# Decay matrices of a chunked scan: dt and the mask moved into the exponent, masking and the sum of both directions on GpSimd

## The chip, the core and the metric

The kernel runs on one core of a Trainium2 chip. A core has five engines that work side by side, each through a queue of its own in a fixed order: TensorE (PE in the profile; PEld is its loading of weights), VectorE (DVE), ScalarE (ACT), GpSimd (POOL) and SyncE (SP), which here only issues transfers. They wait for each other through semaphores. The metric is the device time of one launch in microseconds; less is better.

## The reference, cut to what matters

One layer of a diffusion backbone: 512 latent tokens, 256 context tokens, width 1024, one input projection, a convolution branch, a bidirectional Mamba-2 scan with 32 heads in 8 groups, an output projection and an MLP. The change touches the scan inside chunks of 128 tokens only:

```python
cum = jnp.cumsum(dts * a, axis=2)
xdt = x5 * dts[..., None]
seg = cum_t[..., :, None] - cum_t[..., None, :]
lower = jnp.tril(jnp.ones((q, q), dtype=bool))
decay = jnp.exp(jnp.where(lower, seg, -jnp.inf))
cb = jnp.einsum('bcqgn,bckgn->bcgqk', cs_, bs)
y_diag = jnp.einsum('bcgrqk,bckgrp->bcqgrp', cb[:, :, :, None] * decay, xdt)
...
y_off = jnp.einsum('bcqgn,bcgrpn,bcqgr->bcqgrp', cs_, h_in, jnp.exp(cum))
```

Both directions are added, the backward one with the upper triangle as its mask. For each head and chunk the kernel so needs the matrix M[k, q] = cb[k, q] * sum over the two directions of mask * exp(cum_q - cum_k) * dt_k.

## The kernel before

Tokens lie along the free axis, channels on the partitions. Every large product is done as three passes over exact high and low halves (`gemm`, L114 to L116): a weight tile of 128 columns and all 1024 channels takes 24 products. Its weights come by one transfer (`raw`, L96), ScalarE makes the high half (`whi`, L105), VectorE the low half (`wlo`, L106), with two buffers for each. The tile framework lists the instructions of every engine in an order of priority; `later(n)` moves what is traced inside it. That order is fixed when the program is built: each engine takes its instructions strictly one after the other.

After the conditioning and the first norms, `dt_part` (L294 to L359) computes dt and the running sums cf of dt times a for all 64 head-directions, writes cf and exp(cf) to a scratch in DRAM (`s_cf`), and turns wg, cf and dt to token-by-partition form (`wgT`, `cfT`, `dtT`). Then come eight groups. For group g, `proj(g)` makes B, C, X and Z of the group (six weight tiles; `taps5`, L374, runs the short convolution on VectorE straight out of PSUM), and `ssd(g, ...)` does the scan. Beside groups 0 to 4, `glu` and `taps` run a tile of the convolution branch, whose 30 taps per tile (L575) are all on VectorE. After group 7 come three more of these tiles, the gates, LayerNorm, and the projections.

Inside `ssd`: `cps` holds cb of the four chunks (L442) and VectorE multiplies it with a mask for each direction (`cbm`, L446). B and x are transposed (`bps`, `xps`), x is weighted (`xw`, L470), the states that enter the chunks are built (`sps`, `hst`, L485 to L498). Then for j = 0, 1 there is a pair of heads, r = 0, 1, with one PSUM tile `yps`. For each head and direction d:

- SP fetches cf and exp(cf) of this head, spread over all partitions, into `cfb` (L507, 3 buffers).
- ScalarE makes relu(cf_k - cf_q) chunk by chunk (L510, four instructions; the per-token cf is the bias), and exp(-that) (L512, one instruction) into `e`.
- VectorE multiplies with the masked `cbm` (L513).
- dt: for d = 0 ScalarE scales the four chunks (L517), for d = 1 VectorE multiplies and adds onto the first direction (L520, four instructions). The tile of d = 0 is then M.
- `Cd` = C times exp(cf) (L523): one of four on VectorE, three on GpSimd.

M tiles come from the tag "M" with three buffers, so the fourth head of a group writes where the group's first head stood. TensorE does 16 products of `Cd` and `hst` (L536) and 8 of M and `xt` (L532) for each `yps` tile, each 64 x 128. The two heads of a pair fill the two halves of PSUM's partitions. The trace counts every such f32 product as two instructions, so 32 and 16. What follows is `yt` (L540, L541), its store and its square sum (GpSimd, L548).

Of the kernel before, what the change touches and what calls it, by code (L numbers as in the profile page):

```python
# [8 lines left out]
F32 = mybir.dt.float32  # L9
F32R = mybir.dt.float32r  # L10
BF16 = mybir.dt.bfloat16
AF = mybir.ActivationFunctionType
ALU = mybir.AluOpType
# [13 lines left out]
# columns of the packed per-channel vectors  # L27
# [8 lines left out]
# order of the input projection's 128-column tiles  # L36
# [6 lines left out]
# the groups beside which the first tiles of the convolution module run  # L43
GLU_AT = (0, 1, 2, 3, 4)
# the steps of the first modulation vectors beside which the first three weight tiles come, and ctx
BEGIN_AT, CTX_AT = (0, 1, 2), 3
# products that keep the tensor engine's clock up before there is work
WARM = 22
# the products of C and the decays (direction, head of the pair) that VectorE does, the rest are GpSimd's
DECAYS_V = ((0, 1),)  # L50
# how far instructions move in the order of priority
# [5 lines left out]
def build(tc, xT, ctxT, cond, crow, wada1, wada2, vecs, hv, cst, w_in, w_co, w_so, w_o, w_1, w_2, outT):  # L57
    nc = tc.nc
    with ExitStack() as es:
# [8 lines left out]
        C = cp.tile([P, 4, P], F32, name="C")  # L68
        ident, ones, mask_f, mask_b = (C[:, i, :] for i in range(4))

# [15 lines left out]
        @contextmanager  # L86
        def later(n):
            """what is traced inside gives way to the next n instructions"""
            tc.cur_priority += n
            yield  # L90
            tc.cur_priority -= n

# [37 lines left out]
        def rsqrt_mean(ps, n, cnt, r=None):  # L130
            """1/sqrt(sum/cnt + EPS) of a sum broadcast over the partitions"""
# [18 lines left out]
        def rsqrt_rows(parts, n, cnt, pool, out=None):  # L150
            """the same of the sum of several tiles, found token by token and then spread over the partitions"""
# [40 lines left out]
        with tc.tile_pool(name="st", bufs=1) as st:  # L192
# [31 lines left out]
            # products of nothing: the tensor engine's clock halves when it idles  # L224
# [52 lines left out]
        nc.sync.dma_start(C[:, 2:], cst[:, 2:])  # L277
# [7 lines left out]
        H2 = 2 * HEADS  # L285
        cfT = cp.tile([P, NCH, H2], F32, name="cfT")
        dtT = cp.tile([P, NCH, H2], F32, name="dtT")
# [6 lines left out]
        def dt_part(ps, pc):  # L294
            conv = bigt("conv")
            # rows: heads forward, the same again, heads backward, the same again; the first of each hold
            # chunks 0 to 2, the second chunk 3 and the context
# [10 lines left out]
            # softplus: max(v, 0) + log1p(u), u = exp(-|v|), log1p(u) = 2 atanh(u / (2 + u))  # L308
# [13 lines left out]
            # running sums within the chunks and within the context, backward ones from the end  # L322
# [15 lines left out]
            nc.vector.tensor_tensor(wg, wg, dt_, ALU.mult)  # L338
            nc.scalar.activation(ecf, cf, AF.Exp)
# [5 lines left out]
            # step s: chunk s forward, chunk 3 - s backward  # L345
# [4 lines left out]
            for src, dst in ((wg, wgT), (cf, cfT), (dt_, dtT)):  # L350
                pt = pm.tile([P, T], F32, name="dtp", tag="pm")
                for c in range(3):
                    nc.tensor.transpose(pt[:, c * P:(c + 1) * P], src[:, c * P:(c + 1) * P], ident)
                pv = pt[:, :L].rearrange("p (c d w h) -> p c d w h", c=3, d=2, w=2)
                dv = dst.rearrange("p c (d h) -> p c d h", d=2)
                nc.scalar.copy(dv[:, :3], pv[:, :, :, 0])
                n = dst.shape[1] - 3
                nc.scalar.copy(dv[:, 3:], pv[:, :n, :, 1])
            return conv  # L359

# [26 lines left out]
        def xbc_first():  # L387
            """the first group's, all of x's part before ctx's"""
# [24 lines left out]
        cacc = acct("cacc")  # L413

# [22 lines left out]
        def ssd(g, Bt, Ct, X, Z):  # L437
            ch = lambda t, c: t[:, c * P:(c + 1) * P]
            # B^T C of every chunk, for both directions
# [3 lines left out]
            cbm = []  # L443
            for m in (mask_f, mask_b):
                t = spool.tile([P, NCH, P], F32, name="cbm", tag=f"cbm{len(cbm)}", bufs=1)
                nc.vector.tensor_tensor(  # L446
                    t, cps.rearrange("p (c q) -> p c q", q=P), m.unsqueeze(1).broadcast_to([P, NCH, P]), ALU.mult)
                cbm.append(t)
            # B by token
# [6 lines left out]
            # x by token, and times what reaches the chunk's end  # L456
# [21 lines left out]
            # states that enter the chunks: step s is chunk s forward, chunk 3-s backward  # L478
# [20 lines left out]
            # outputs of the heads, two to a PSUM tile  # L499
            for j in range(2):  # L500
                yps = py.tile([P, T], F32, name="yps", tag="py")
                Ms, Cs = [], ([], [])
                for r in range(2):
                    for d in range(2):
                        hd = d * HEADS + 4 * g + 2 * j + r
                        cb_ = spool.tile([P, 2, T], F32, name="cfb", tag="cfb", bufs=3)
                        nc.sync.dma_start(cb_, s_cf[hd].unsqueeze(0).broadcast_to([P, 2, T]))  # L507
                        e = (spool if d else tp).tile([P, T], F32, name="e", tag="e" if d else "M", bufs=2 if d else 3)
                        for c in range(NCH):
                            nc.scalar.activation(  # L510
                                ch(e, c), cb_[:, 0, c * P:(c + 1) * P], AF.Relu, bias=cfT[:, c, hd:hd + 1], scale=-1.0)
                        nc.scalar.activation(e, e, AF.Exp, scale=-1.0)  # L512
                        nc.vector.tensor_tensor(e, e, cbm[d].rearrange("p c q -> p (c q)"), ALU.mult)  # L513
                        if d == 0:
                            M = e
                            for c in range(NCH):
                                nc.scalar.activation(ch(M, c), ch(M, c), AF.Copy, scale=dtT[:, c, hd:hd + 1])  # L517
                        else:
                            for c in range(NCH):
                                nc.vector.scalar_tensor_tensor(  # L520
                                    ch(M, c), ch(e, c), dtT[:, c, hd:hd + 1], ch(M, c), ALU.mult, ALU.add)
                        Cd = (spool if d else tp).tile([P, T], F32, name="Cd", tag="Cd", bufs=4 if d else 3)
                        (nc.vector if (d, r) in DECAYS_V else nc.gpsimd).tensor_tensor(Cd, Ct, cb_[:, 1, :], ALU.mult)  # L523
                        Cs[d].append(Cd)
                    Ms.append(M)
# [178 lines left out]
        def four_w(srcs, hpool, lpool, name):  # L704
            """four weight tiles that stay"""
# [10 lines left out]
        def sumsq(j, a, b, wcol):  # L716
            """squares of channel tile j added up; the last tile's by themselves"""
# [9 lines left out]
        def with_norm(srcs, rhs, gcol, keep, finish, wcol=None):  # L727
            """x1 += gate * product; the last four tiles by halves of the tokens, so that each half's
            norm runs beside the next products"""
# [74 lines left out]
def _layout(inp):  # L804
# [33 lines left out]
    i = np.arange(P)  # L838
    cst = np.stack([np.eye(P), np.ones((P, P)), i[:, None] <= i[None, :], i[:, None] >= i[None, :]], 1)
# [37 lines left out]
```

## Time and profile before

Three timed runs: 1263.3, 1263.39 and 1267.06 us, median 1263.39. The profiled execution has a span of 1264.2 us from its first to its last instruction; no other time of that execution is given.

| what | value |
|---|---|
| median of the timed runs | 1263.39 us |
| span of the profiled execution | 1264.2 us |
| mean granted TensorE clock | 0.991 |
| scan with the group projections (about 100 to 620 us) | 520 us |
| GpSimd in it | 67 instructions, 102.6 us busy |
| loads of ScalarE's function tables, L512 alone | 28, 35.9 us |

A row of a group of instructions reads: line, engine, operation, tile written <- tiles read, shapes, count | busy time, mean ns of one | idle time of the engine just before them, with what ended it. In a timeline a row is: start, duration, engine, line, operation, count, and in brackets the idle time before it and what ended that. A busy TensorE is not TensorE at its peak, since products are pipelined: how dense it is can be read from the distance of the starts, not from the durations.

### The profile page before, as it was taken

What the parts mean: (1) busy time and instruction counts of PE and PEld (TensorE: products, weight loads), DVE (VectorE), ACT (ScalarE), POOL (GpSimd) and SP (SyncE); (2) the same over time, 40 slices, a digit from 0 to 9 for tenths busy, and PEclk for the clock granted to TensorE, in tenths of its full rate; (3) what the DMA queues carried; (4) which work ended last, traced back from release to release, by engine and by line L of the source; (5) the groups of instructions that cost most, each with busy time, mean ns of one, the idle gap of its engine ahead of it and who ended that gap; (6) DMA issues with size and microseconds to landing.
All of it is one profiled execution on the core that took longest, in us unless ns stands there. A gap on an engine that the chain in (4) does not pass through costs nothing.

```text
span 1264.2 us, 17493 instructions
## 1 busy us (share of the span) xinstructions
PE 1220.7 (97%) x6665; PEld 995.6 (79%) x6665; DVE 953.7 (75%) x1567; ACT 667.4 (53%) x1124; POOL 108.9 (9%) x74
## 2 busy tenths in 40 slices
PE   6998999999999899999999999999999999999997
PEld 3786778777787778787888877778998888888886
DVE  6797689999999999998999798885843343443444
ACT  4557888686776748868453452134431331331442
POOL 0001222121020302124000000000000000000000
PEclk8999999999999999999999999999999999999999
DMA  9424363343342424333363357964222333233332
GB/s 363 142 67 133 137 198 128 120 146 106 121 159 93 158 83 147 112 134 117 109 193 126 119 188 258 305 196 153 62 65 86 100 100 92 92 100 101 96 104 67
DMA packets 56260, 169.96 MB, mean 134 GB/s; under 512 B 6640, under 2 KB 9584, under 8 KB 56048
## 3 DMA queue, kind: packets, MB, share of 16 engines
q1 hardware_dynamic: 56176, 168.85, 41.0%
q8 instruction: 52, 0.85, 0.3%
q14 instruction: 32, 0.26, 0.1%
HBM read 162.27 MB, written 6.55 MB: 134 GB/s over the span
## 4 chain that ended last, share of the span: by engine, by line
PE 65%; DVE 20%; DMA 8%; issue 3%; ACT 3%; SPq 0%; POOL 0%; DVEq 0%; ACTq 0%; POOLq 0%
PE ps L114 20%; PE ps L115 19%; PE ps L116 19%; DVE conv L575 5%; DVE wlo L106 3%; DVE Xt L374 3%; DMA aw<-in_wada_dram 2%; DMA cfb<-s_cf 2%; PE yps L536 2%; PE yps L532 2%; PE sps L485 1%; DMA yr<-s_y 1%; DVE aw L675 1%; DMA raw<-in_w_dram 1%; ACT whi L105 1%
## 5 line engine op out<-in xcount | busy, mean ns | idle before, releaser
L105 ACT CAST whi<-raw 128x1024 fp32r<-128x1024 f32 x163 | 170.9, 1049 | 320.6 <-PE ps L115 291.5
L106 DVE TENSOR_TENSOR wlo<-raw,whi 128x1024 fp32r<-128x1024 f32 x163 | 203.8, 1251 | 84.3 <-ACT whi L105 76.1
L114 PE MATMUL ps<-hh,whi 128*128 128x512 f32 x632 | 258.0, 408 | 2.3 <-DVE Xt L374 2.1
L116 PE MATMUL ps<-hh,wlo 128*128 128x512 f32 x632 | 255.4, 404 | 2.3 <-DVE wlo L106 2.2
L115 PE MATMUL ps<-hl,whi 128*128 128x512 f32 x632 | 256.7, 406 | 0.0
L575 DVE SCALAR_TENSOR_TENSOR conv<-sg,V,conv 128x480 f32<-128x480 f32 (+14 forms) x240 | 173.3, 740 | 2.6 <-ACT conv L569 1.1
L114 PEld LDWEIGHTS ps<-hh,whi 128*128 128x128 f32 x632 | 119.4, 189 | 30.8 <-issue 7.2
L116 PEld LDWEIGHTS ps<-hh,wlo 128*128 128x128 f32 x632 | 119.4, 189 | 30.7 <-DVE wlo L106 4.7
L115 PEld LDWEIGHTS ps<-hl,whi 128*128 128x128 f32 x632 | 119.6, 189 | 26.5 <-issue 3.7
L711 DVE SCALAR_TENSOR_TENSOR x<-ps,mod,x 128x512 f32<-128x512 f32 (+1 forms) x48 | 31.7, 660 | 100.1 <-PE ps L116 100.1
L510 ACT ACTIVATE e<-cfb,cfT 128x128 f32<-128x128 f32 x256 | 83.9, 391 | 36.8 <-PE yps L532 17.5
L523 POOL TENSOR_TENSOR Cd<-Ct,cfb 128x512 f32<-128x512 f32 x48 | 72.6, 1518 | 313.0 <-DMA cfb<-s_cf 250.3
L116 PE MATMUL ps<-h2h,wlo 128*128 128x512 f32 (+1 forms) x240 | 89.8, 375 | 0.0
L115 PE MATMUL ps<-h2l,whi 128*128 128x512 f32 (+1 forms) x240 | 89.8, 375 | 0.0
L114 PE MATMUL ps<-h2h,whi 128*128 128x512 f32 (+1 forms) x240 | 89.4, 375 | 0.0
L115 PE MATMUL ps<-gl,whi 128*128 128x512 f32 x224 | 88.4, 395 | 0.0
L114 PE MATMUL ps<-gh,whi 128*128 128x512 f32 x224 | 88.2, 394 | 0.0
L116 PE MATMUL ps<-gh,wlo 128*128 128x512 f32 x224 | 87.9, 392 | 0.0
L374 DVE SCALAR_TENSOR_TENSOR Xt<-ps,V,Xt 128x255 f32<-128x255 f32 (+3 forms) x128 | 74.2, 605 | 3.9 <-ACT Xt L370 3.6
L114 PE MATMUL ps<-hc,whi 128*128 128x256 f32 x184 | 52.5, 285 | 3.1 <-DVE Xt L374 3.1
L115 PE MATMUL ps<-hc,whi 128*128 128x256 f32 x184 | 52.4, 285 | 0.0
L116 PE MATMUL ps<-hc,wlo 128*128 128x256 f32 x184 | 52.1, 283 | 0.0
(259 smaller groups left out, 2417.5 us busy)
## 6 DMA issues: line engine op xcount, KB each, us to landing
raw<-in_w_in_dram SPq DMA_DIRECT2D x81, 512.0 KB, 3.6
cfb<-s_cf SPq DMA_DIRECT2D x64, 512.0 KB, 4.4
raw<-in_w_dram SPq DMA_DIRECT2D x64, 512.0 KB, 3.5
aw<-in_wada_dram SPq DMA_DIRECT2D x64, 256.0 KB, 4.3
ablk<-in_wada_dram SPq DMA_DIRECT2D x16, 512.0 KB, 8.6
raw<-in_w_so_dram SPq DMA_DIRECT2D x16, 512.0 KB, 3.7
s_y<-yt SPq DMA_DIRECT2D x16, 256.0 KB, 2.2
yr<-s_y SPq DMA_DIRECT2D x16, 256.0 KB, 3.6
```

What stands on the lines that cost most here:

```text
L105: nc.scalar.copy(hi, raw)
L106: nc.vector.tensor_tensor(lo, raw, hi, ALU.subtract)
L114: nc.tensor.matmul(ps, lhsT=whi[:, k, :], rhs=rhi[:, k, t0:t1], start=start and k == 0, stop=False)
L115: nc.tensor.matmul(ps, lhsT=whi[:, k, :], rhs=rlo[:, k, t0:t1], start=False, stop=False)
L116: nc.tensor.matmul(ps, lhsT=wlo[:, k, :], rhs=rhi[:, k, t0:t1], start=False, stop=stop and k == KT - 1)
L374: nc.vector.scalar_tensor_tensor(o[:, lo:hi], ps[:, lo + d:hi + d], vcol(V_SCW + 5 * ch + j), o[:, lo:hi], ALU.mult, ALU.add)
L510: nc.scalar.activation(ch(e, c), cb_[:, 0, c * P:(c + 1) * P], AF.Relu, bias=cfT[:, c, hd:hd + 1], scale=-1.0)
L523: (nc.vector if (d, r) in DECAYS_V else nc.gpsimd).tensor_tensor(Cd, Ct, cb_[:, 1, :], ALU.mult)
L532: nc.tensor.matmul(o, lhsT=xt[:, c, hr, :], rhs=ch(Ms[r], c), start=False, stop=True, skip_group_check=True)
L536: nc.tensor.matmul(o, lhsT=hst[:, s, k, hr * 64:hr * 64 + 64], rhs=ch(Cs[k][r], c), start=k == 0 and c == 0, stop=False, skip_group_check= ...
L575: nc.vector.scalar_tensor_tensor(o[:, :, lo:hi], u[:, :, lo + d:hi + d], wv(j), o[:, :, lo:hi], ALU.mult, ALU.add)
L711: nc.vector.scalar_tensor_tensor(x1[:, j, a:b], ps[:, a:b], mod[:, gcol + j, 0:1], x1[:, j, a:b], ALU.mult, ALU.add)
```

## The change

The mask constants go, and with them `cbm`: `cb` is one plain copy of `cps` by ScalarE. In `dt_part` three instructions are added (a floor of 1e-18 under dt, ln dt, minus cf), so that one transposed tile `bT` = ln dt - cf takes the place of `cfT` and `dtT`. For each head and direction GpSimd now writes -1e30 into the masked triangle of the fetched cf (`affine_select`, L514 of the changed kernel, in place in `cfb`), and ScalarE makes mask * dt_k * exp(cf_q - cf_k) in four instructions Exp(cf_q + bT) (L518). GpSimd adds the two directions (L525), and VectorE multiplies the sum with `cb` (L526), once for each head.

```diff
-        C = cp.tile([P, 4, P], F32, name="C")
+        C = cp.tile([P, 2, P], F32, name="C")
...
             nc.vector.tensor_tensor(wg, wg, dt_, ALU.mult)
+            nc.vector.tensor_scalar(dt_, dt_, DT_MIN, None, ALU.max)
+            nc.scalar.activation(dt_, dt_, AF.Ln)
+            nc.vector.tensor_tensor(dt_, dt_, cf, ALU.subtract)
             nc.scalar.activation(ecf, cf, AF.Exp)
...
-            for src, dst in ((wg, wgT), (cf, cfT), (dt_, dtT)):
+            for src, dst in ((wg, wgT), (dt_, bT)):
...
+        never = nc.gpsimd.to_reg(NEVER)
...
-            cbm = []
-            for m in (mask_f, mask_b):
-                t = spool.tile([P, NCH, P], F32, name="cbm", tag=f"cbm{len(cbm)}", bufs=1)
-                nc.vector.tensor_tensor(
-                    t, cps.rearrange("p (c q) -> p c q", q=P), m.unsqueeze(1).broadcast_to([P, NCH, P]), ALU.mult)
-                cbm.append(t)
+            cb = spool.tile([P, T], F32, name="cb", tag="cb", bufs=1)
+            nc.scalar.copy(cb, cps)
...
+                        x3 = cb_[:, 0, :].rearrange("p (c q) -> p c q", q=P)
+                        sign = -1 if d else 1
+                        nc.gpsimd.affine_select(x3, x3, pattern=[[0, NCH], [sign, P]], compare_op=ALU.is_ge,
+                                                fill=never, base=0, channel_multiplier=-sign)
                         e = (spool if d else tp).tile([P, T], F32, name="e", tag="e" if d else "M", bufs=2 if d else 3)
                         for c in range(NCH):
                             nc.scalar.activation(
-                                ch(e, c), cb_[:, 0, c * P:(c + 1) * P], AF.Relu, bias=cfT[:, c, hd:hd + 1], scale=-1.0)
-                        nc.scalar.activation(e, e, AF.Exp, scale=-1.0)
-                        nc.vector.tensor_tensor(e, e, cbm[d].rearrange("p c q -> p (c q)"), ALU.mult)
-                        if d == 0:
-                            M = e
-                            for c in range(NCH):
-                                nc.scalar.activation(ch(M, c), ch(M, c), AF.Copy, scale=dtT[:, c, hd:hd + 1])
-                        else:
-                            for c in range(NCH):
-                                nc.vector.scalar_tensor_tensor(
-                                    ch(M, c), ch(e, c), dtT[:, c, hd:hd + 1], ch(M, c), ALU.mult, ALU.add)
+                                ch(e, c), cb_[:, 0, c * P:(c + 1) * P], AF.Exp, bias=bT[:, c, hd:hd + 1])
+                        es_.append(e)
                         Cd = (spool if d else tp).tile([P, T], F32, name="Cd", tag="Cd", bufs=4 if d else 3)
...
+                    M = es_[0]
+                    nc.gpsimd.tensor_tensor(M, M, es_[1], ALU.add)
+                    nc.vector.tensor_tensor(M, M, cb, ALU.mult)
                     Ms.append(M)
```

The framework lists the instructions anew, so their order changes on every engine. Line numbers of the changed kernel are 2 to 3 higher: L117 to L119 are the large products, L538 and L534 the products with `Cd` and with M.

TensorE, group 3, before: the end of the first pair of heads. `yps<-e,xt` is a product with M, `ps` a large product.

```order
L114 MATMUL ps<-hh,whi 128x512
L532 MATMUL yps<-e,xt 64x128 x2
L115 MATMUL ps<-hl,whi 128x512
L116 MATMUL ps<-hh,wlo 128x512
L532 MATMUL yps<-e,xt 64x128 x2
L114 MATMUL ps<-hh,whi 128x512
L115 MATMUL ps<-hl,whi 128x512
L116 MATMUL ps<-hh,wlo 128x512
L532 MATMUL yps<-e,xt 64x128 x2
L114 MATMUL ps<-hh,whi 128x512
L115 MATMUL ps<-hl,whi 128x512
L532 MATMUL yps<-e,xt 64x128
```

The same place after the change, with all products of both pairs of the group:

```order
L119 MATMUL ps<-hh,wlo 128x512
L538 MATMUL yps<-Cd,hst 64x128 x16
L534 MATMUL yps<-e,xt 64x128 x8
L538 MATMUL yps<-Cd,hst 64x128 x16
L534 MATMUL yps<-e,xt 64x128
L117 MATMUL ps<-hh,whi 128x512
L118 MATMUL ps<-hl,whi 128x512
L119 MATMUL ps<-hh,wlo 128x512
L534 MATMUL yps<-e,xt 64x128 x7
L117 MATMUL ps<-hh,whi 128x512
```

What stood in pieces among the large products now stands in two pieces; groups 1 to 5 show the same rows. Counted over the whole program, the products into `yps` stand in 65 pieces between others before and in 23 after. Before, between the last product with the first head's M and the first with the fourth head's M of a group (which share a buffer) TensorE has more than the work of a whole large tile (24 products) to do; after, in groups 1 to 5, there are one product with M, 16 with `Cd`, one more with M, and three large ones, and about as much in groups 6 and 7.

GpSimd, about group 3, before (`yacc` and `cacc` are running sums):

```order
L523 TENSOR_TENSOR Cd<-Ct,cfb 128x512 x4
L580 TENSOR_TENSOR cacc<-cacc,conv 128x512
L548 TENSOR_TENSOR yacc<-yacc,ysq 128x512
L523 TENSOR_TENSOR Cd<-Ct,cfb 128x512 x4
L548 TENSOR_TENSOR yacc<-yacc,ysq 128x512
```

GpSimd for the same group after. `e<-e` is the sum of the two directions.

```order
L522 TENSOR_TENSOR Cd<-Ct,cfb 128x512 x2
L514 AFFINE_SELECT cfb<-cfb 128x512
L522 TENSOR_TENSOR Cd<-Ct,cfb 128x512
L514 AFFINE_SELECT cfb<-cfb 128x512
L522 TENSOR_TENSOR Cd<-Ct,cfb 128x512
L514 AFFINE_SELECT cfb<-cfb 128x512
L522 TENSOR_TENSOR Cd<-Ct,cfb 128x512
L525 TENSOR_TENSOR e<-e 128x512
L514 AFFINE_SELECT cfb<-cfb 128x512 x2
L522 TENSOR_TENSOR Cd<-Ct,cfb 128x512
L525 TENSOR_TENSOR e<-e 128x512
```

Every `cfb` buffer now passes through GpSimd before ScalarE may read it, and each head's M as well. Behind the last row stand two more selects, for the next group, and then the sum of the group's fourth head.

VectorE at the end of group 3 after the change:

```order
L564 TENSOR_TENSOR sg<-sg,ps 128x512
L109 TENSOR_TENSOR wlo<-raw,whi 128x1024
L522 TENSOR_TENSOR Cd<-Ct,cfb 128x512
L577 SCALAR_TENSOR_TENSOR conv<-sg,V,conv 128x8x49
L542 SCALAR_TENSOR_TENSOR yt<-Xt,V,yps 128x512
L577 SCALAR_TENSOR_TENSOR conv<-sg,V,conv 128x8x50
L543 TENSOR_TENSOR yt<-yt,Z 128x512
L526 TENSOR_TENSOR e<-e,cb 128x512
```

The last row is the product for the fourth head's M; before, this head had a product with `cbm` for each direction (L513) and four instructions of L520 at this place.

More of the change, by code (lines that the diff above doesn't have):

```diff
@@ L25 @@
 CK = 31
+NEVER, DT_MIN = -1e30, 1e-18
+CFB = 3
 V_N1, V_N2, V_FN = 0, 8, 16
@@ L67, in build @@
         V = cp.tile([P, NV], F32, name="V")
-        C = cp.tile([P, 4, P], F32, name="C")
-        ident, ones, mask_f, mask_b = (C[:, i, :] for i in range(4))
+        C = cp.tile([P, 2, P], F32, name="C")
+        ident, ones = (C[:, i, :] for i in range(2))
         def bigt(name, dt=F32, shape=(P, KT, T)):
@@ L276, in build @@
         nc.sync.dma_start(V[:, V_SNW:], vecs[:, V_SNW:])
-        nc.sync.dma_start(C[:, 2:], cst[:, 2:])
         c_k = lambda k: ctx[k // 2][:, k % 2, :]
@@ L285, in build @@
         H2 = 2 * HEADS
-        cfT = cp.tile([P, NCH, H2], F32, name="cfT")
-        dtT = cp.tile([P, NCH, H2], F32, name="dtT")
+        bT = cp.tile([P, NCH, H2], F32, name="bT")
         wgT = cp.tile([P, NCH + 2, H2], F32, name="wgT")
@@ L503, in ssd @@
                 for r in range(2):
+                    es_ = []
                     for d in range(2):
                         hd = d * HEADS + 4 * g + 2 * j + r
-                        cb_ = spool.tile([P, 2, T], F32, name="cfb", tag="cfb", bufs=3)
+                        cb_ = spool.tile([P, 2, T], F32, name="cfb", tag="cfb", bufs=CFB)
                         nc.sync.dma_start(cb_, s_cf[hd].unsqueeze(0).broadcast_to([P, 2, T]))
+                        x3 = cb_[:, 0, :].rearrange("p (c q) -> p c q", q=P)
+                        sign = -1 if d else 1
+                        nc.gpsimd.affine_select(x3, x3, pattern=[[0, NCH], [sign, P]], compare_op=ALU.is_ge,
+                                                fill=never, base=0, channel_multiplier=-sign)
                         e = (spool if d else tp).tile([P, T], F32, name="e", tag="e" if d else "M", bufs=2 if d else 3)
@@ L837, in _layout @@
             inp["conv_dw_w"][0].reshape(CK, 8, P).transpose(2, 1, 0).reshape(P, -1)]
-    i = np.arange(P)
-    cst = np.stack([np.eye(P), np.ones((P, P)), i[:, None] <= i[None, :], i[:, None] >= i[None, :]], 1)
+    cst = np.stack([np.eye(P), np.ones((P, P))], 1)
     return {
```

## The prediction

> **What bounds the kernel now.** I read the page's first part, then the busy time by stretches, then TensorE's waits in the scan.
>
> ```profile
> PE 1220.7 (97%) x6665; PEld 995.6 (79%) x6665; DVE 953.7 (75%) x1567; ACT 667.4 (53%) x1124; POOL 108.9 (9%) x74
> 200.00:300.00 100.00, 96.99 (x547) 78.33 (x547) 96.75 (x148) 74.36 (x131) 23.68 (x15) 1.00 0.41 137
> 300.00:400.00 100.00, 99.14 (x585) 79.13 (x584) 97.23 (x161) 68.01 (x126) 11.90 (x9) 1.00 0.35 114
> 400.00:500.00 100.00, 95.79 (x572) 78.44 (x571) 95.59 (x153) 70.52 (x134) 18.69 (x13) 0.98 0.38 120
> 620.00:1264.00 644.00, 631.53 (x3078) 527.77 (x3076) 397.69 (x637) 229.19 (x308) 6.53 (x3) 1.00 0.41 129
> ```
>
> The columns after the length are PE, PEld, DVE, ACT, POOL, the granted clock, the DMA share and GB/s. In the scan TensorE and VectorE are both at 96 to 99%; behind it VectorE is at 62% and TensorE alone is full. So a gain must come out of the scan, and only as far as TensorE gets through it sooner. Its visible waits there (100 to 620 us):
>
> ```profile
> PE yps L536 <- POOL Cd L523: 6.2, 3, 3.1
> PE ps L114 <- DVE Xt L374: 3.4, 2, 2.1
> PE ps L116 <- DVE wlo L106: 2.1, 3, 0.9
> PE sps L485 <- DVE xw L470: 1.2, 2, 0.8
> PE xps L465 <- DVE cbm L446: 1.1, 1, 1.1
> PE yps L536 <- DVE hst L498: 1.1, 3, 0.5
> PE yps L536 <- DVE Cd L523: 1.0, 2, 0.7
> PE yps L532 <- DVE e L520: 0.6, 2, 0.4
> ```
>
> VectorE accounts for 10.5 us, GpSimd for 6.2. That is little: 99.6 us of VectorE's work (below) can't come back as 99.6 us of time.
>
> **The change part by part: VectorE, ScalarE and GpSimd.** The groups touched:
>
> ```profile
> L513 DVE TENSOR_TENSOR e<-e,cbm 128x512 f32<-128x512 f32 x64 | 46.6, 731 | 2.3 <-ACT e L512 2.3
> L520 DVE SCALAR_TENSOR_TENSOR e<-e,dtT 128x128 f32<-128x128 f32 x128 | 42.6, 358 | 0.2
> L446 DVE TENSOR_TENSOR cbm<-cps,C 128x512 f32<-128x512 f32 x16 | 10.4, 682 | 1.6 <-PE cps L442 1.4
> L512 ACT ACTIVATE e<-e 128x512 f32<-128x512 f32 x64 | 40.1, 627 | 0.6
> L517 ACT ACTIVATE e<-e,dtT 128x128 f32<-128x128 f32 x128 | 41.3, 392 | 7.8 <-DVE e L513 7.6
> L523 POOL TENSOR_TENSOR Cd<-Ct,cfb 128x512 f32<-128x512 f32 x48 | 72.6, 1518 | 313.0 <-DMA cfb<-s_cf 250.3 <-ACT Ct L384 55.9 <-PE ps L116 6.8
> ```
>
> VectorE loses 46.6 + 42.6 + 10.4 = 99.6 us and gains 32 products at 0.731, 23.4: 76 us less. ScalarE loses 81.4; its Exp with a per-token bias takes the place of the Relu one for one, and the eight copies of `cb` are at most 8 x 0.63 = 5 us. At 68 to 75% it doesn't set the pace, so I count nothing for it; if it did, this would be a gain. The three added instructions in `dt_part` are cheap beside transfers that group 0 waits for anyway: nothing.
>
> GpSimd gets 32 sums at 1.52, 49 us, and 64 selects, which no row shows. One reads a single 128x512 operand where L523 reads two; the bounds are nothing much and twice L523, 3.0 us; I take 1.0, nearer to the row of its own size. That makes 113 us on top of 102.6, in 520 us: no limit by throughput. The Trainium skill ("GPSIMD Engine Reference", 4.1) calls one-input work there "roughly line-rate", at 1.2 GHz an estimate of 0.43 us for a select; the sum below would come out 2 us lower. No run here shows it.
>
> But GpSimd's work is not free for VectorE:
>
> ```profile
> L106 DVE TENSOR_TENSOR wlo<-raw,whi x57: 1207/1216/2054, 100.4 to 617.8; 128x1024 fp32r<-128x1024 f32 x57
> L106 DVE TENSOR_TENSOR wlo<-raw,whi 128x1024 fp32r<-128x1024 f32 x57 | 74.5, 1307 | 1.6 <-ACT whi L105 1.2
> L513 DVE TENSOR_TENSOR e<-e,cbm x64: 673/682/1783, 116.4 to 602.7; 128x512 f32<-128x512 f32 x64
> ```
>
> (ns: least, median, most.) The medians are 7% under the means of 1307 and 731, and the longest take 0.8 to 1.1 us more: instructions with two operands in SBUF sometimes stand still, by about what one of GpSimd's lasts. 7% of VectorE's 290 us in the three quoted stretches is 20 us, beside 54 us of GpSimd: 0.37 per us, an upper bound if not every instruction in the 290 can be held up so. For 113 us of new work that is 42, and 34 of the 76 stay: VectorE falls from 97% to about 90%. I take half of its 10.5 us of waits as gone: **-5** (bounds 0 and -10.5).
>
> **TensorE's order.** Its work is the same, but cut up less (65 pieces of `yps` products, now 23), and a piece costs something by itself:
>
> ```profile
> 321.27 1.31 PE L536 MATMUL yps<-Cd,hst 128*64 128x128 f32 x20
> 322.41 0.38 PE L532 MATMUL yps<-e,xt 128*64 128x128 f32 x2
> ...
> 325.37 0.39 PE L116 MATMUL ps<-hh,wlo 128*128 128x512 f32 x1
> 325.59 0.39 PE L114 MATMUL ps<-hh,whi 128*128 128x512 f32 x1
> 325.91 0.44 PE L532 MATMUL yps<-e,xt 128*64 128x128 f32 x4
> 326.28 0.50 PE L115 MATMUL ps<-hl,whi 128*128 128x512 f32 x1
> 326.62 0.40 PE L116 MATMUL ps<-hh,wlo 128*128 128x512 f32 x1
> ```
>
> By starts, 20 small ones take 1.14 us, 0.057 each, and a large one 0.225 (325.37 to 325.59). From 325.59 to 326.62 stand two large and four small ones: 0.45 + 0.23 = 0.68, but it took 1.03. So one piece costs 0.34 us more than its products. 42 pieces fewer: **-14.3** (the other end is 0, if TensorE only waits instead).
>
> **The new wait.** The fourth head's M is written where the first head's stood. Behind the last product with that one, TensorE now has a last product with M (0.11), 32 small ones as the trace counts them (1.82), one with M (0.11), three large ones (0.68) and 0.1 for the switch: 2.8 us, then it needs the fourth M. In that time the chain has to run: four Exp, the sum on GpSimd, the product on VectorE.
>
> ```profile
> 392.33 1.28 ACT L510 ACTIVATE e<-cfb,cfT 128x128 f32<-128x128 f32 x4 [0.58 <-DVE e L520]
> ```
>
> 1.28 + 1.52 + 0.73, and four hand-overs at 0.05 (128.50 + 1.27 to 129.82, below): 3.7 us, 0.9 too late. Behind the sum waits VectorE's product, and behind that, in VectorE's queue, the taps and the second `yt`; nothing that TensorE needs soon. Ahead of it stand four instructions, three of them with two SBUF operands, so I add one collision, 0.73: 1.6 us. In groups 1 to 7: **+11**. The ends: 1.27 and 0.68 without any collision, 0.6 each, +4; a further sum's and product's time, 3.1 each, +22.
>
> Whether such waits also cost clock:
>
> ```profile
> 436.81 0.47 PE L114 MATMUL ps<-hh,whi 128*128 128x512 f32 x1 [2.12 <-DVE Xt L374]
> 438.84 0.69 PE L116 MATMUL ps<-hh,wlo 128*128 128x512 f32 x1 [0.88 <-DVE wlo L106]
> 439.33 0.63 PE L114 MATMUL ps<-hh,whi 128*128 128x512 f32 x1
> 439.75 0.63 PE L115 MATMUL ps<-hl,whi 128*128 128x512 f32 x1
> ```
>
> After 2.12 and 0.88 us of idling close together the large products start 0.42 apart, and the granted clock of 400 to 500 us is 0.98 (2 us lost). A wait of 1.65 (129.82, below) stands alone; I count nothing, with +11 as the far end (seven times eight products at 0.2). The Trainium skill ("TensorE: Matmul & The Clock Gate", Part 1) lets the clock fall only after an idle window of about 3.4 us; by that rule none of the seven waits costs clock and the sum stands, though here 3.0 us with work between was enough.
>
> **Group 0** starts when the first `cfb` have come:
>
> ```profile
> 113.69 0.43 PE L536 MATMUL yps<-Cd,hst 128*64 128x128 f32 x2 [3.15 <-POOL Cd L523]
> 121.21 7.15 DMA cfb<-s_cf
> 128.50 1.27 POOL L523 TENSOR_TENSOR Cd<-Ct,cfb 128x512 f32<-128x512 f32 x1 [9.64 <-DMA cfb<-s_cf]
> 129.82 0.43 PE L536 MATMUL yps<-Cd,hst 128*64 128x128 f32 x2 [1.65 <-POOL Cd L523]
> ```
>
> Both waits end with a transfer and then GpSimd's `Cd`. Now a select stands ahead of each `Cd`: **+1** for the first. For the second, the buffer is freed sooner (one pass of ScalarE instead of two over M) but passes GpSimd first; I call it even (bounds -2 and +8, all eight selects in a row).
>
> **The sum**: -5 - 14.3 + 11 + 1 = -7.3 us. The profiled span, 1264.2, is 0.8 over the median of the runs, 1263.39; so 1256.9 of span, **1256** by the median.
>
> **Rivals.**
>
> *GpSimd too slow for its place* (slower). If the select lasts over 1.5 us, all terms turn: per us more, 64 x 0.37 = 24 us of VectorE's gain go (at 3.0 us VectorE is fuller than before: about +5 us of TensorE's waits for each us), a select of the next group stands ahead of the fourth head's sum (+7), and half of group 0's eight show (+4). 16 us per us against a gain of 7.3: the point is 1.5 us. At 2.2 us it gives 1275, at 3.0 1288. For it: L523's 1.52 for two operands, and nothing shows the select. Against it: one operand, and GpSimd idle four fifths of the scan. 0.25.
>
> *The gain is waited away* (no change). VectorE is as full as TensorE, and if collisions give back all 76 us, TensorE comes sooner to products whose operands come no sooner: -14.3 turns to about -4, -5 to 0, the fourth head's +11 is partly the same waiting, so that +4 (its lower end) to +11 of it are added, and +1 stays: +1 to +8, 1264 to 1271. 0.17, a third of it over 1267.2.
>
> *The fourth head is in time*: no collisions, 0.6 us a group, and all of VectorE's waits gone: -10.5 - 14.3 + 4 + 1 = -20, 1243. The wait is worked out from few rows; against it, VectorE's four instructions ahead. 0.13.
>
> **How the numbers follow.** The forecast, from 1248 to 1263, has 0.45, and holds gains over 0.3% (3.8 us, about what a measurement of this kernel can tell from no change) up to 1259.6: 0.37 of the 0.45. Faster: 0.37 + 0.13 = 0.50. Same: 0.08 and 0.11 of the no-change case: 0.19. Slower: 0.25 and 0.06: 0.31. The range goes from 1243 to 1278: it leaves out a still larger gain and a select near 3 us.
>
> **What would show it.** Right: VectorE at about 90% between 200 and 500 us; the `yps` products in two bursts per group; TensorE waiting 1 to 2 us per group at the product with the fourth head's M, released by VectorE's product with `cb`; selects at about 1 us; seven waits, clock at 1.00. Wrong: selects over 1.5 us, TensorE's waits for `Xt` and `wlo` longer than before, or VectorE still at 97%.

## The result: 0.7% slower, and the profile after

Over 20 runs each, the changed kernel takes 1273.68 us (median) and the kernel before 1263.74; the ratio is 1.0067, 95% interval 1.0054 to 1.0081. The forecast was 1256 and faster; the time lies within the range of 1243 to 1278, on its slow side. The profiled execution took 1273.29, with a span of 1271.4, 7.2 us more than before. The profiled execution of the kernel before was one of its slower ones: elsewhere the span is 1.8 to 2.0 us under the time, which makes it about 1266, so the spans lie closer together than the medians. The page's first part and the stretches of the scan:

```profile
PE 1213.4 (95%) x6662; PEld 1002.7 (79%) x6662; DVE 923.8 (73%) x1393; ACT 610.8 (48%) x948; POOL 214.8 (17%) x170
200.00:300.00 100.00, 96.54 (x563) 81.20 (x562) 93.68 (x129) 67.50 (x108) 41.80 (x33) 0.98 0.41 137
300.00:400.00 100.00, 93.32 (x582) 77.03 (x581) 90.39 (x120) 60.45 (x106) 39.65 (x29) 0.97 0.38 124
400.00:500.00 100.00, 96.68 (x566) 81.93 (x565) 93.16 (x130) 58.04 (x92) 35.65 (x26) 0.98 0.36 120
620.00:1264.00 644.00, 636.12 (x3100) 532.02 (x3099) 397.79 (x632) 230.37 (x309) 8.26 (x3) 1.00 0.41 129
```

VectorE did fall, from 96 to 97% to 90 to 94%, and ScalarE too. But TensorE is no busier, and its granted clock, 1.00 in two of these three stretches before, is now 0.97 to 0.98. TensorE's waits from 100 to 640 us, longest total first:

```profile
PE yps L534 <- DVE e L526: 15.7, 7, 2.4
PE sps L487 <- DVE xw L472: 5.3, 4, 3.5
PE sps L487 <- ACT hst L493: 4.1, 1, 4.1
PE ps L119 <- DVE wlo L109: 2.9, 4, 1.2
PE xps L467 <- ACT cb L450: 1.7, 5, 0.8
```

The first row is the wait for the fourth head's M, seven times, as the prediction placed it, but 2.2 us of idling each instead of 1.6 (2.4 by the starts of the products). The chain behind one of them, in the timelines of ScalarE, GpSimd, VectorE and TensorE:

```profile
246.56 2.45 ACT L518 ACTIVATE e<-cfb,bT 128x128 f32<-128x128 f32 x8 [1.23 <-PE yps L534]
247.92 3.27 POOL L525 TENSOR_TENSOR e<-e 128x512 f32<-128x512 f32 x2 [9.03 <-ACT e L518]
250.00 1.74 DVE L526 TENSOR_TENSOR e<-e,cb 128x512 f32<-128x512 f32 x1 [1.18 <-POOL e L525]
249.00 0.39 PE L119 MATMUL ps<-hh,wlo 128*128 128x512 f32 x1
251.79 1.57 PE L534 MATMUL yps<-e,xt 128*64 128x128 f32 x14 [2.40 <-DVE e L526]
253.29 0.80 PE L117 MATMUL ps<-hh,whi 128*128 128x512 f32 x1
253.88 0.63 PE L118 MATMUL ps<-hl,whi 128*128 128x512 f32 x1
254.31 0.63 PE L119 MATMUL ps<-hh,wlo 128*128 128x512 f32 x1
```

TensorE's last product with the first head's M frees the slot, and ScalarE starts at 246.56. The first four of its eight Exp are the fourth head's; the other four already belong to the next group. GpSimd's first sum runs from 247.92 to about 249.96, and VectorE's product from 250.00 to 251.74, while GpSimd is in the second sum, that of the next group. TensorE goes on at 251.79. From 253.88 the large products start 0.43 us apart instead of 0.23: the clock is halved.

The sum of TensorE's lost time, worked out from the starts of all its products between 100 and 640 us (the distance of two starts less the product's own 0.227 us for 512 columns, 0.054 for a small one as the trace counts it; over 0.3 us a wait, below it switching between shapes; what falls to a halved clock apart):

| us lost from 100 to 640 us | before | after | difference | predicted |
|---|---|---|---|---|
| first product with an M | 0.9 | 16.9 | +16.0 | +11 |
| switching, pieces among it | 34.6 | 17.7 | -16.9 | -14.3 |
| waits in group 0's start | 5.1 | 5.9 | +0.8 | +1 |
| other waits (evictions, `wlo`, `xps`, `sps`, `Cd`) | 14.6 | 14.1 | -0.5 | -5 |
| halved clock | 3.2 | 10.8 | +7.6 | 0 |
| sum | 58.4 | 65.4 | +7.0 | -7.3 |

So the 7.2 us of the span are all in the scan, and these are the terms to explain. From the forecast's -7.3 to the +7.0 it is 14.3 us: 7.6 of clock, 5.0 more for the fourth head and 4.5 for the other waits, less 2.6 for the pieces and 0.2 for group 0.

### The profile page after: what moved, and what is told of

Read it like the earlier page. It is cut to its first block, busy times and chain, and to the rows that moved or that the text cites. A ratio compares the mean times of both kernels' runs of the same rounds, so it can differ in the third digit from the quotient of the medians.

```text
span 1271.4 us, 17342 instructions
## 1 busy us (share of the span) xinstructions
PE 1213.4 (95%) x6662; PEld 1002.7 (79%) x6662; DVE 923.8 (73%) x1393; ACT 610.8 (48%) x948; POOL 214.8 (17%) x170
## 4 chain that ended last, share of the span: by engine, by line
PE 53%; DVE 20%; DMA 9%; ACT 8%; issue 8%; POOL 2%; SPq 0%; DVEq 0%; ACTq 0%; POOLq 0%
PE ps L117 17%; PE ps L119 16%; PE ps L118 16%; DVE conv L577 6%; DMA cfb<-s_cf 3%; DVE wlo L109 3%; DVE e L526 2%; DMA aw<-in_wada_dram 2%; ACT whi L108 1%; ACT e L518 1%; PE sps L487 1%; ACT L518 1%; DVE aw L677 1%; DVE Bt L379 1%; POOL e L525 1%
## 5 line engine op out<-in xcount | busy, mean ns | idle before, releaser
L119 PE MATMUL ps<-hh,wlo 128*128 128x512 f32 x632 | 255.3, 404 | 3.2 <-DVE wlo L109 3.2
L117 PE MATMUL ps<-hh,whi 128*128 128x512 f32 x632 | 257.8, 408 | 0.1
L577 DVE SCALAR_TENSOR_TENSOR conv<-sg,V,conv 128x392 f32<-128x392 f32 (+14 forms) x240 | 187.0, 796 | 2.6
L119 PEld LDWEIGHTS ps<-hh,wlo 128*128 128x128 f32 x632 | 120.0, 190 | 32.3 <-DVE wlo L109 6.6
L117 PEld LDWEIGHTS ps<-hh,whi 128*128 128x128 f32 x632 | 120.2, 190 | 27.6 <-issue 3.4
L518 ACT ACTIVATE e<-cfb,bT 128x128 f32<-128x128 f32 x256 | 82.4, 391 | 46.7 <-POOL cfb L514 26.2
L119 PE MATMUL ps<-h2h,wlo 128*128 128x512 f32 (+1 forms) x240 | 89.8, 375 | 0.0
L117 PE MATMUL ps<-h2h,whi 128*128 128x512 f32 (+1 forms) x240 | 89.4, 375 | 0.0
L117 PE MATMUL ps<-gh,whi 128*128 128x512 f32 x224 | 88.2, 394 | 0.0
L119 PE MATMUL ps<-gh,wlo 128*128 128x512 f32 x224 | 87.9, 392 | 0.0
L379 DVE SCALAR_TENSOR_TENSOR Xt<-ps,V,Xt 128x510 f32<-128x510 f32 (+3 forms) x128 | 75.0, 607 | 9.8 <-ACT Xt L375 9.2
L514 POOL TENSOR_SCALAR_AFFINE_SELECT cfb<-cfb 128x512 f32<-128x512 f32 x64 | 49.9, 781 | 187.2 <-DMA cfb<-s_cf 179.5
L525 POOL TENSOR_TENSOR e<-e 128x512 f32<-128x512 f32 x32 | 52.2, 1638 | 86.3 <-ACT e L518 84.5
L487 PE MATMUL sps<-xw,Bk 128*128 128x256 f32 x160 | 47.1, 401 | 10.0 <-DVE xw L472 5.3
```

The source lines that it names most:

```text
L117: nc.tensor.matmul(ps, lhsT=whi[:, k, :], rhs=rhi[:, k, t0:t1], start=start and k == 0, stop=False)
L119: nc.tensor.matmul(ps, lhsT=wlo[:, k, :], rhs=rhi[:, k, t0:t1], start=False, stop=stop and k == KT - 1)
L379: nc.vector.scalar_tensor_tensor(o[:, lo:hi], ps[:, lo + d:hi + d], vcol(V_SCW + 5 * ch + j), o[:, lo:hi], ALU.mult, ALU.add)
L487: nc.tensor.matmul(ps[:, d * 256:(d + 1) * 256], lhsT=ch(Bk, c), rhs=xw[d][:, wi[d](c)].rearrange("p h e -> p (h e)"), start=i == 0, stop= ...
L514: nc.gpsimd.affine_select(x3, x3, pattern=[[0, NCH], [sign, P]], compare_op=ALU.is_ge, fill=never, base=0, channel_multiplier=-sign)
L518: nc.scalar.activation(ch(e, c), cb_[:, 0, c * P:(c + 1) * P], AF.Exp, bias=bT[:, c, hd:hd + 1])
```

## The experiments

Ratios are to the kernel before in the same batch of runs; the change itself has 1.0067. Two theories stood against each other at first. A: the fourth head's wait and the clock that it costs have eaten the gain. B: GpSimd's doubled load holds VectorE up, so TensorE waits in one place if not in another.

### Four buffers for M

```diff
-tag="e" if d else "M", bufs=2 if d else 3
+tag="e" if d else "M", bufs=2 if d else 4
```

> The buffers of M go from 3 to 4, nothing else; the fourth head's Exp no longer wait for the first head's last product. Theory A (the fourth head's wait and the clock it costs are what ate the gain): the seven waits of 16.9 us in all and the five half-clock stretches behind them (1.7 us each, 8.5) go, so about 1273.7 - 25 = 1248 us, ratio to before 0.988, yps waits for the product with cb under 2 us, clock 1.00 from 200 to 500 us. Theory B (GpSimd's doubled load holds VectorE up, and TensorE waits for VectorE in one place if not in another): the waits move to xw, Xt and wlo, 1268 us or more, ratio 1.003 or more.

1262.92 us, ratio 1.0002 (0.9983 to 1.0020): by the ratios 8 us of the 25, between the two. The wait at the fourth head is gone, and half-clock stretches fell from seven to three in the scan, but new rows took their place:

```profile
PE sps L487 <- DVE xw L472: 6.2, 7, 2.6
PE ps L119 <- DVE wlo L109: 5.8, 8, 0.8
PE xps L467 <- ACT cb L450: 4.4, 5, 1.6
PE ps L117 <- DVE Bt L379: 2.7, 3, 1.1
PE yps L534 <- DVE e L526: 1.7, 1, 1.7
```

Counted as in the table, "first product with an M" is 1.9, the clock 4.9, but the waits for projections are 13.9 (4.3 in the change). A is right about its 16 us, and they are not simply to be had: behind them stands something else. The same buffer was not tried in the kernel before, which has no 2 KB per partition left for it.

### The sum on VectorE

```diff
-nc.gpsimd.tensor_tensor(M, M, es_[1], ALU.add)
+nc.vector.tensor_tensor(M, M, es_[1], ALU.add)
```

> The sum of the two directions on VectorE instead of GpSimd (32 sums of 0.68 us there instead of 32 of 1.64 on GpSimd), three buffers of M as in the change. Theory A: four Exp, sum and product take 1.36 + 0.68 + 0.68 and two hand-overs, 2.9 us, and eight or nine large products instead of three now stand ahead of the fourth M, 4.1 us of cover: the seven waits go as with four buffers, about 1250 us. Theory B: 52 us less of GpSimd give VectorE 0.37 x 52 = 19 us back, and 22 us of sums come on: no change, about 1273 us.

1258.73 us, ratio 0.9965 (0.9948 to 0.9982): faster than both kernels. The wait for the fourth M is 1.6 us in all, and one half-clock stretch is left. The page's first part, in this run and in the change with four M buffers:

```profile
PE 1204.2 (96%) x6662; PEld 995.3 (79%) x6662; DVE 924.0 (74%) x1425; ACT 613.5 (49%) x950; POOL 166.9 (13%) x138
PE 1207.6 (96%) x6662; PEld 997.7 (79%) x6662; DVE 924.2 (73%) x1393; ACT 609.3 (48%) x948; POOL 214.7 (17%) x170
```

VectorE is as busy as in the change (924.0 us for 923.8): the 22 us of sums that it took over came back elsewhere, as B had counted. But the time fell by 13 us by the ratios where B had said no change, so VectorE's load alone doesn't set it; and it is still 9 us above A's 1250.

### Every select twice

```diff
 nc.gpsimd.affine_select(x3, x3, ...)
+nc.gpsimd.affine_select(x3, x3, ...)
```

> Every select is made twice, which changes no value: 64 x 0.78 = 50 us more on GpSimd. Theory A: no select stands ahead of the fourth head's sum, so the seven waits stay at 2.4 us; group 0 shows some of its eight selects (0.64 each): 1274 to 1279 us. Theory B, and the price of the prediction's rival (16 us for each us that a select lasts longer): 0.78 x 16 = 12 us and more, 1286 us or above, with VectorE standing still 0.37 x 50 = 18 us more.

1285.29 us, ratio 1.0173 (1.0143 to 1.0202): B's number. But not by B's mechanism, as the waits of ScalarE in the change and then, in this run, the page's first part, the same waits and two of TensorE's show (lines are two further down here, L520 the Exp, L516 the second select, L528 the product with `cb`):

```profile
ACT e L518 <- POOL cfb L514: 26.2, 9, 4.3
```

```profile
PE 1217.3 (95%) x6662; PEld 1006.6 (78%) x6662; DVE 923.9 (72%) x1393; ACT 610.7 (48%) x948; POOL 262.7 (20%) x234
ACT e L520 <- POOL cfb L516: 60.4, 29, 5.2
PE yps L536 <- DVE e L528: 20.7, 8, 3.6
PE xps L467 <- ACT cb L450: 4.6, 5, 1.6
```

GpSimd has 48 us more to do, and VectorE is no busier for it (923.9 us for 923.8). ScalarE's Exp wait 34 us longer for the select, 29 times instead of 9. ScalarE takes its instructions in order, so the casts (`whi`) and copies (`cb`) behind such an Exp start later too. Neither theory had that: the select is a new link between every transfer and ScalarE.

### TensorE kept busy in the wait

```diff
+NFILL = 10
...
+if j and r and c == 0:
+    for _ in range(NFILL):
+        nc.tensor.matmul(yps[64:, :], lhsT=zero[:, :64], rhs=zero, start=False, stop=False, ...)
```

> Ten products with a zero operand (128x512 bf16, about 0.22 us each, 2.2 us) stand on TensorE ahead of the fourth head's first product in every group, so that TensorE is busy during the wait and the wait itself stays. If the idling behind the wait is what halves the clock: no half-clock stretch behind the waits of groups 2 to 6, -8.5 us, +2.2 in group 0, which has no wait there: about 1267 us. If the clock falls for another reason, or costs nothing: 1274 to 1276 us, with the half-clock stretches still there.

1268.35 us, ratio 1.0040 (1.0022 to 1.0058), where 1267 was expected; by the ratios 3 us came back of the 6 expected, and the two intervals overlap a little. The fill stands where the wait was, and the products behind it run at full clock:

```profile
249.51 2.32 PE L539 MATMUL yps<-zero 128*64 128x512 bf16 x10
251.76 0.50 PE L118 MATMUL ps<-hh,whi 128*128 128x512 f32 x1
252.10 0.40 PE L119 MATMUL ps<-hl,whi 128*128 128x512 f32 x1
252.98 1.09 PE L541 MATMUL yps<-e,xt 128*64 128x128 f32 x14 [0.48 <-DVE e L529]
253.99 0.50 PE L120 MATMUL ps<-hh,wlo 128*128 128x512 f32 x1
254.33 0.40 PE L118 MATMUL ps<-hh,whi 128*128 128x512 f32 x1
254.56 0.39 PE L119 MATMUL ps<-hl,whi 128*128 128x512 f32 x1
```

In the whole scan one half-clock stretch is left, at group 0, and every timed run has a mean clock of 0.990 or more (0.978 to 0.990 in the change). So the idling itself halves the clock, and that was a real part of the loss, though its size is clearer from the table than from this run's time.

### What relief of VectorE is worth

The same edit in the kernel before and in the change with four M buffers:

```diff
-if d == 0:
+if d == 0 or (t < 5 and j % 2):
     continue
```

> The kernel before, with every other tap of the convolution module's first five tiles left out (75 of 150, about 0.66 us each: 50 us less for VectorE in the scan, nothing else taken away; its output lacks those taps). The order of TensorE then has 46 pieces of yps products instead of 66. If relief of VectorE is worth what the prediction counted (half to all of its 10.5 us of waits, and 20 pieces at 0.34, 6.8 us): 1246 to 1251 us. If TensorE is held up by the order of VectorE's queue and not by its load: the pieces alone, 1256 us. If relief is worth nothing: 1263 us.

1251.1 us, ratio 0.9904 (0.9872 to 0.9937): the prediction's price holds, at its low end. Waits for evictions and weights fell from 6.7 us to 0.9, switching from 34.6 to 25.6. With 20 pieces fewer the first products with an M wait here too, 6.8 us where it was 0.9.

> The change with four buffers of M (1263 us), and the same 75 taps left out: 50 us less for VectorE. If VectorE's load has taken the place of the fourth head's wait: its 14 us of waits for weights and evictions and 8 us for xw shrink to less than half, 1250 us or below. If the new waits come from where instructions stand in VectorE's queue (M's products ahead of xw, behind cb and behind GpSimd's sum): no more than 4 us, 1259 us or above.

1254.29 us, ratio 0.9928 (0.9902 to 0.9953): 9 us, in between. The waits for `xw` are all but gone, but these stay, larger than with all taps:

```profile
PE xps L467 <- ACT cb L450: 8.7, 6, 1.8
PE ps L119 <- DVE wlo L109: 8.7, 11, 1.6
```

The first hangs on ScalarE's copy. Ahead of each late `cb` ScalarE had worked for 7 us or more without a pause, with two or three loads of its function tables (1.28 us each) among the work. The second doesn't hang on ScalarE: at all eleven waits `whi` had been ready for 0.6 to 5.2 us, and VectorE, 77% full from 200 to 500 us, came to `wlo` without a pause from the instructions ahead of it in its queue. So VectorE's load is a part of what followed the fourth head's wait, and the order of VectorE's queue and ScalarE's lateness are others.

### No selects, and selects that nobody waits for

Both have four M buffers and leave the decays unmasked; the Exp has a scale and a bias with which these don't overflow. In the first the select's line is simply gone; in the second it writes a tile of its own:

```diff
-nc.gpsimd.affine_select(x3, x3, ...)
+nc.gpsimd.affine_select(scr, x3, ...)
...
-AF.Exp, bias=bT[:, c, hd:hd + 1])
+AF.Exp, bias=wgT[:, c, hd:hd + 1], scale=1e-3)
```

> Four buffers of M, and all 64 selects left out (the decays are then not masked, and the Exp takes a small scale and another bias, so that no value overflows): 57 us less for GpSimd, VectorE's and ScalarE's work as it was. Doubling the selects cost 11.6 us for 57 us more on GpSimd, 0.2 us per us. If GpSimd's load costs the same downwards (VectorE's instructions standing still, chains through GpSimd being late): 1251 us. If it only costs where it lengthens a chain that is waited for, and four buffers have taken that chain away: 1261 us or above.

1244.99 us, ratio 0.9856 (0.9825 to 0.9888): 18 us less than with selects, more than doubling them had cost.

> As the run without selects (four buffers of M, unmasked decays, 1245 us), but all 64 selects are made, into a tile that nobody reads: GpSimd's load is that of the change, its selects still read the transfer's buffer, and only the Exp no longer wait for them. If the selects cost through the chain (ScalarE's Exp wait for them, 21.7 us in 9 waits, with casts and copies for TensorE queued behind): 1245 to 1250 us, ScalarE's waits for GpSimd gone. If they cost through GpSimd's load (VectorE's instructions standing still, Cd and sums later): 1259 us or above. Half and half: about 1254.

1250.06 us, ratio 0.9880 (0.9841 to 0.9919). Of the 18 us, 15 are saved with GpSimd still doing all 64 selects, as long as no Exp waits for them; the last 3 lie within the intervals. This run's page and ScalarE's two longest waits:

```profile
PE 1205.4 (96%) x6662; PEld 999.0 (80%) x6662; DVE 922.7 (74%) x1393; ACT 611.7 (49%) x948; POOL 215.2 (17%) x170
ACT whi L108 <- PE ps L118: 55.3, 24, 4.3
ACT e L519 <- DMA cfb<-s_cf: 28.0, 13, 3.3
```

GpSimd and VectorE are as busy as with four buffers and the selects in place (215.2 and 922.7 us for 214.7 and 924.2). No wait of an Exp for GpSimd stands among ScalarE's any more; there it was "ACT e L518 <- POOL cfb L514", 21.7 us in 9 waits. So nearly all of what the selects cost is where they stand, not their load.

### What a piece costs

Four M buffers, and a zero product put between the small ones:

```diff
+if k and c and r:
+    nc.tensor.matmul(yps, lhsT=zero, rhs=hh[:, 0, :], start=False, stop=False, ...)
```

> Four buffers of M, and 96 products with a zero operand (128x512, as large as the projections') put between the small yps products, 12 in each group's two bursts by six: each cuts a burst once more and takes about 0.227 us itself, 21.8 us. If a piece costs what the prediction took (0.34 us beside its products): 96 x 0.34 = 33 us more, in all +54 on 1263, 1317 us, and in the trace 0.55 to 0.6 us from one small product to the next over a zero product. If the pieces cost nothing by themselves and their time in the trace of before was waiting: +22, 1285 us.

1301.6 us (two runs), ratio 1.0309 (1.0264 to 1.0354), between the two forecasts, but the trace is clear:

```profile
262.46 0.44 PE L543 MATMUL yps<-Cd,hst 128*64 128x128 f32 x4
262.83 0.49 PE L536 MATMUL yps<-hh,zero 128*128 128x512 f32 x1
263.26 0.44 PE L543 MATMUL yps<-Cd,hst 128*64 128x128 f32 x4
263.62 0.49 PE L536 MATMUL yps<-hh,zero 128*128 128x512 f32 x1
```

From 262.83 to 263.26 it takes 0.43 us from a zero product to the next small one, and from 262.46 to 262.83 0.37 for four small ones, 0.15 more than 4 x 0.054. Over all 96 the medians are 0.425 and, from the last small one on, 0.202: together 0.627, of which the two products' own time is 0.281. So a piece costs 0.35 us. The 96 cost TensorE 55 us, and the time rose by 39: the rest came out of what was lost anyway, since TensorE's waits and halved clock are about 40 us with four M buffers alone and 26 in this run.

### Versions that combine what helped

Sum on VectorE, four M buffers, and a second quarter of `Cd` on VectorE (`DECAYS_V = ((0, 1), (1, 0))`):

> Four buffers of M, the sum on VectorE, and 16 more of the Cd products on VectorE (32 of 64): GpSimd loses 52 and 25 us, VectorE gets 22 and 11. If GpSimd's load costs 0.25 us per us (0.2 from doubled selects, 0.3 from none) and VectorE's 0.2 (11 us for 50): -19 and +7, about 1251 us, beside 1258.7 for the sum alone. If VectorE at 97% is again what TensorE waits for: 1258 us or above.

1254.82 us, ratio 0.9933 (0.9912 to 0.9955): 4 us beyond the sum alone (0.9965, the intervals overlap), where the price by load had forecast 8. ScalarE still waits 33.2 us for selects in it.

Sum on VectorE and four buffers for the decays (`CFB = 4`), three for M:

> The sum on VectorE (1258.7 us), three buffers of M, and four buffers instead of three for the decays that come from memory, so that a transfer and its select can run one head and direction earlier. If ScalarE's waits for transfers and selects (27 and 26 us there) are what holds its queue, with the casts behind: they fall to under half, and about 1250 us. If it is GpSimd's load and not the select's place: 1257 to 1260 us.

1252.9 us, ratio 0.9908 (0.9882 to 0.9935): 7 us under the sum alone, without any load taken off GpSimd. "ACT e L518 <- POOL cfb L514", 26.5 us with three buffers, is no longer among the longest waits; those for the transfer itself stay (27.1 there, 23.2 here):

```profile
ACT L518 <- DMA cfb<-s_cf: 23.2, 7, 3.9
PE yps L534 <- DVE e L526: 5.0, 5, 1.2
```

The same with the second quarter of `Cd` on VectorE:

> The sum on VectorE and four buffers for the decays (1252.9 us), and 16 more Cd products on VectorE: 25 us less for GpSimd, 11 more for VectorE, none of them between a transfer and an Exp that is waited for once the buffers are there. If GpSimd's load itself costs (0.25 us per us): -6 + 2, 1249 us. If it costs only where it stands in a chain, as the selects into an unread tile say (a quarter of their price left): -1 to +2, 1252 to 1255 us.

1250.7 us, ratio 0.9910 (0.9888 to 0.9932): the same as without, so taking 25 us off GpSimd, for 11 more on VectorE, is worth nothing that can be measured once the Exp no longer wait for it. Both are about 0.9% faster than the kernel before and 1.6% faster than the change.

## Why the prediction was wrong, step by step

**Shown right.** VectorE's busy time fell by 30 us over the whole execution (953.7 to 923.8), near the 34 that were left of the 76 after collisions. (From 100 to 620 us it fell by just 34, 476.6 to 442.5, but the changed scan ends 7 us later.) The group of the selects:

```profile
L514 POOL TENSOR_SCALAR_AFFINE_SELECT cfb<-cfb 128x512 f32<-128x512 f32 x64 | 49.9, 781 | 187.2 <-DMA cfb<-s_cf 179.5
```

One takes 0.78 us in the mean, for the 1.0 taken (the shortest 0.63, so the estimate of 0.43 is too low), so the condition of the slower rival (over 1.5) was not met, and its direction came all the same. The pieces: -16.9 with all switching, for -14.3, and a piece at 0.35 us measured alone (the prediction's rows give 0.35 too, where it wrote 0.34).

**Right in size alone: group 0, +0.8 for +1.** The two waits for `Cd`, 4.8 us before, are down to 1.2. In their place TensorE waits 4.1 us at `sps` for ScalarE's copy `hst`, which stands in ScalarE's queue behind the first Exp, and these behind the transfer. That the two come out nearly even is luck.

**The step that failed most: "Whether such waits also cost clock", which counted nothing.** The term was 0 with +11 as its far end; it measured +7.6. The argument was that a wait of 1.65 us that stood alone had cost none. Stretches of 3.4 us of the change, one with a fourth-head wait inside and the next, then two that another such wait lies across:

```profile
248.80:252.20 3.40, 1.00 (x11) 0.57 (x11) 2.23 (x3) 0.73 (x2) 3.40 (x3) 1.00 0.83 205
252.20:255.60 3.40, 3.40 (x18) 2.59 (x14) 3.37 (x5) 0.99 (x3) 1.54 (x2) 0.51 0.11 40
177.10:180.50 3.40, 1.93 (x23) 1.28 (x19) 2.23 (x4) 2.07 (x7) 2.94 (x2) 1.00 0.78 209
180.50:183.90 3.40, 2.48 (x20) 2.08 (x21) 3.37 (x4) 0.44 (x2) 2.69 (x3) 1.00 0.42 161
```

TensorE was busy for 1.00 of the first 3.4 us, and the next 3.4 ran at half clock. The wait that begins near 179 us is as long (2.38 for 2.40), but lies across the two, which were busy for 1.93 and 2.48, and cost no clock. Five of the seven waits did, at 1.7 us each; one more new half-clock stretch follows the wait of 3.54 us for `xw` below. The Trainium skill ("TensorE: Matmul & The Clock Gate", Part 1) has the clock judged in free-running windows of 3.4 us, with which these traces agree: their half-clock stretches start whole multiples of 3.413 us apart. The prediction had weighed its rule that one idle window is needed, and here a window idle for 2.40 of the 3.4 us was enough.

**The term that was mis-sized: the fourth head, "1.28 + 1.52 + 0.73" and one collision of 0.73, +11.** It measured +16.0. The place, the count and the cover of 2.8 us were right (2.83 from 246.56 to where TensorE stops, at 251.79 - 2.40). The chain took 5.23 us, not 4.4: the sum 2.04 for 1.52, the product 1.74 for 0.73. One collision was put in, and there were two. The second was not bad luck:

```profile
L526 DVE TENSOR_TENSOR e<-e,cb x32: 674/1736/1792, 118.1 to 596.8; 128x512 f32<-128x512 f32 x32
```

The median of the new product is 1736 ns where the shortest takes 674: GpSimd ends one head's sum, VectorE starts its product, and GpSimd's next instruction, a sum for the next group or (in the last two groups) one into `yacc`, which was queued right behind, holds it. Of the 32 products, 12 take 674 to 692 ns with no two-operand instruction of GpSimd beside them, and 17 take 1735 to 1792 beside such a one. So the collision was built into the order, and the trace of before had no such pair to show it. The Trainium skill ("SBUF — State Buffer", "Who interferes with whom") gives a pair of ports that VectorE and GpSimd share under an exclusive lock, and says that a VectorE instruction with two SBUF inputs contends there with a GpSimd instruction that reads SBUF; the two groups of durations fit that.

**The term that vanished: VectorE's waits, -5.** That relief by itself is worth something is shown by the half taps (50 us less, 11 us faster). But TensorE's waits for `xw` rose from 1.2 us to 5.3 (rows above and in the prediction) and gave most of it back. The prediction had said that nothing TensorE needs soon is queued behind the product with `cb`. That is true of the fourth head only. At a group's start, two products with `cb` for its heads stand ahead of `xw`, here at the longest of the four waits, in the timelines of VectorE, GpSimd and TensorE:

```profile
517.42 3.46 DVE L526 TENSOR_TENSOR e<-e,cb 128x512 f32<-128x512 f32 x2
520.80 3.13 DVE L472 TENSOR_TENSOR xw<-xps,wgT 128x512 f32<-128x512 f32 x6
518.62 1.71 POOL L525 TENSOR_TENSOR e<-e 128x512 f32<-128x512 f32 x1
522.22 4.14 PE L487 MATMUL sps<-xw,Bk 128*128 128x256 f32 x11 [3.54 <-DVE xw L472]
```

Each product there takes 1.75 to 1.78 us, beside GpSimd's sums, and TensorE waits 3.54 us for the `xw` behind. At the three other waits (0.5 to 0.7 us) two products of 1.8 us stand ahead in the same way.

**The cost that no rival had: the select between transfer and Exp.** ScalarE was counted at nothing because it isn't full. It isn't, but it is in order: its Exp wait 26.2 us for GpSimd, with casts and copies behind that TensorE needs. With four M buffers this link is worth 15 of the 18 us that the selects cost, and with the sum on VectorE a fourth `cfb` buffer, which loosens it, is worth 7. In the table it stands nowhere by itself. That it is part of why the other waits didn't fall in the change, and of why taking away the fourth head's wait and its clock gave only 8 of 25 us, is argued from these runs: the select was not moved aside with three M buffers, and by which of TensorE's waits it costs was not followed (ahead of the late copies `cb` ScalarE was working, not standing at a select).

**The rivals.** "The gain is waited away" came nearest in mechanism (1264 to 1271, at 0.17), but put it down to VectorE's collisions. The time that came is its upper end and 3 us more, and 7.6 us of clock are in it that this rival didn't have. That the time lies within the stated range is luck: the slow end stood there for a slow select (1275 us at 2.2 us each), and the select took 0.78. What stays open: how the waits of the version with four M buffers divide between VectorE's load, the order of its queue and ScalarE's lateness. The halved taps and the selects moved aside gave 9 and 15 us, each alone; both together weren't tried. The two runs with other decays also have another order on TensorE (15 and 16 pieces for 18), at most 1 us by the price of a piece. Every version here was listed anew by the framework, and what another order on the other engines does to its time was not told apart.

## What to carry to other kernels

An operation that moves to an idle engine is priced by its place before its load: ask what it now stands between, which strict queue waits behind it, and what its own engine starts next to its consumer. Where a short burst takes the place of scattered work, count the cover that is left for the buffer that is reused last, and give it one buffer more before counting on the gain. Here a wait that left TensorE idle for more than about half of one clock window of 3.4 us cost its own length and 1.7 us beyond.

## What the runs showed of the hardware that was not expected

All 33 half-clock stretches in the scans of the fourteen traces last 3.41 us or twice that, and within one trace their starts lie whole multiples of 3.413 us apart (in the change 252.25, 323.93, 395.61, 467.29 and 538.97: 21 of them each time). The group of the change takes 71.7 us, nearly 21 windows, so that once one fourth-head wait fell inside a window the next ones did as well. Among the windows of that grid that ran at full clock TensorE had to be idle for about half: up to 1.62 us never halved the next one, from 1.88 on always did, and between them it went either way. Four of the 33 stretches went on for a second window, after 0.33 to 0.88 us of idling in the first.
